# Differential attention and retention with paired score tiles: two products in one two-bank PSUM tile, one VectorE operation for both

## The chip, the core and the metric

The kernel runs on one core of a Trainium2 chip as one program. The metric is the device time of one execution in microseconds (us). The core has five engines with queues of their own: TensorE (matmuls, PE in the profile, its weight loads PEld), VectorE (DVE), ScalarE (ACT), GpSimd (POOL) and SyncE (SP, which issues most of the transfers). Matmuls write to PSUM, eight banks of 128 partitions by 512 float32 elements; VectorE and ScalarE read them from there. A wait between engines goes by semaphore.

## The reference

Two transformer blocks over 512 tokens of width 1024. The first has stick-breaking attention, a gated linear scan and a mixture of 16 experts; the second has retention and differential attention side by side, cross attention and a feed-forward layer. The change touches the second block's mixer alone. Cut to that:

```python
def retention_chunkwise(q, k, v):            # 8 heads, 64 wide, chunks of 128
    scores = einsum('bhncd,bhnjd->bhncj', qc, kc) * dmask      # gamma^(row-column), 0 above the diagonal
    o_intra = einsum('bhncj,bhnjv->bhncv', scores, vc)
    ...                                       # states of earlier chunks, with the same decay
def diff_attention_causal(q, k, v, lam):     # 4 heads, two maps m of 64 each, values 128 wide
    def block(args):                          # a block of 128 queries
        s = einsum('bhmqd,bhmkd->bhmqk', q_blk, k) * scale
        s = where(kpos[None, :] <= qpos[:, None], s, -inf)
        p = softmax(s, axis=-1)
        a = p[:, :, 0] - lam * p[:, :, 1]
        return einsum('bhqk,bhkd->bhqd', a, v)
```

Both results are normalized by head, scaled and multiplied by w_out_2.

## The kernel before

The body is written as one straight program; a scheduler then sets the order of the instructions on each engine, by its own estimate of when operands and buffers are ready, and puts in the semaphores. So projections written behind a head in the program stand between that head's operations on TensorE's queue.

A projection (ws or ts, L192 to L250) takes 512 KB of weights. SP loads them into one of three wraw buffers, ScalarE rounds them to whi (L169), VectorE forms the remainder wlo (L170), and TensorE multiplies three times for each 128 rows of the contraction (L187, L188, L189), into one of two PSUM banks with the tag mm. Sums over squares for the norms are matmuls with ones (L306).

PSUM is split for the whole program: two banks mm, two banks tp, four banks at (L109 and L110). The mixer of the second block runs in two parts.

- diff_head(h), L1175 to L1209, four times. For each of four blocks i of 128 queries, with n = 128(i+1) keys: for each of the two maps m, a score product of 64 partitions into its own bank (L1182), where map 0 has partitions 0 to 63 of query and key and map 1 has 64 to 127; a matmul of the identity with the mask, both bfloat16, which adds -1e30 above the diagonal in the same bank (L1184); the maximum (L1186), its negation (L1187), the exponential with its sum on ScalarE (L1189), the reciprocal (L1190). Then the two maps are weighted and subtracted (L1193, L1194), transposed into another bank (L1197), copied to SBUF (L1199) and multiplied with the values (L1201).
- ret_pair(t), L1256 to L1279, four times, two heads each. For each of four chunks of keys j: two score products, one head in partitions 0 to 63 and one in 64 to 127 (L1266), each multiplied by its decay on VectorE (L1269), and two products with the values (L1271), which write output partitions 0 to 63 and 64 to 127.

float32 matmuls such as these show as two records each in the profile. Queries, keys and values sit in slot2 tiles, 16 buffers with one tag. The rotary step of retention (L1232 to L1240) swaps halves by transfer (sw) and multiplies on VectorE.

Of the kernel before, what the change touches and what calls it, by code (L numbers as in the profile page):

```python
# [8 lines left out]
F32 = mybir.dt.float32  # L9
F32R = mybir.dt.float32r  # L10
BF = mybir.dt.bfloat16
U8 = mybir.dt.uint8
I32 = mybir.dt.int32
AF = mybir.ActivationFunctionType
OP = mybir.AluOpType
AX = mybir.AxisListType.X
PSUM = bass.MemoryType.PSUM
# [3 lines left out]
S = 512  # L21
# [62 lines left out]
def body(tc, a, out):  # L84
# [21 lines left out]
    ps = pool("ps", 1, space=PSUM)  # L106
    dp = pool("dp", 1, space=DRAM)

    def psum(tag, name="ps"):  # L109
        return ps.tile([128, 512], F32, name=name, tag=tag, bufs={"mm": 2, "at": 4, "tp": 2}[tag])  # L110

# [190 lines left out]
    def sums(tag, ones, *sq):  # L302
        w = sq[0].shape[1]
        m = psum(tag)[:, :w]
        for i, q in enumerate(sq):
            T.matmul(m, ones, q, start=(i == 0), stop=(i == len(sq) - 1))  # L306
        return m
# [41 lines left out]
    order(V.tensor_copy(negsb, cs("neg_sb")), last_lo[0])  # L349
    negdf = cp.tile([128, 128], BF, name="negdf")  # L350
    order(V.tensor_copy(negdf, cs("neg_df")), last_lo[0])
# [781 lines left out]
    def slot2(name, dt=F32):  # L1133
        return mp.tile([128, S], dt, name=name, tag="s2", bufs=16)

# [3 lines left out]
    def tmp_(name, bufs):  # L1139
        return tb.tile([128, S], F32, name=name, tag=name, bufs=bufs)  # L1140

    w2 = a["w_in_2"][0]
# [32 lines left out]
    def diff_head(h):  # L1175
        oT = psum("tp")
        for i in range(4):
            n = 128 * (i + 1)
            pp, st = [], []
            for m in range(2):  # L1180
                o = psum("at")[:, :n]
                T.matmul(o, dqn[h][64 * m:64 * m + 64, i * 128:(i + 1) * 128], dkn[h][64 * m:64 * m + 64, :n],  # L1182
                         start=True, stop=False)
                T.matmul(o[:, n - 128:], identb, negdf, start=False, stop=True)  # L1184
                mx_ = sp.tile([128, 3], F32, name="dmx", bufs=6)
                V.reduce_max(mx_[:, 0:1], o, axis=AX)  # L1186
                V.tensor_scalar(mx_[:, 0:1], mx_[:, 0:1], -1.0, None, op0=OP.mult)  # L1187
                p = tmp_("pp", 4)[:, :n]
                A.activation(p, o, AF.Exp, bias=mx_[:, 0:1], accum_out=mx_[:, 1:2])  # L1189
                V.reciprocal(mx_[:, 2:3], mx_[:, 1:2])  # L1190
                pp.append(p)
                st.append(mx_)
            V.tensor_scalar(pp[1], pp[1], st[1][:, 2:3], lam, op0=OP.mult, op1=OP.mult)  # L1193
            V.scalar_tensor_tensor(pp[0], pp[0], st[0][:, 2:3], pp[1], op0=OP.mult, op1=OP.subtract)  # L1194
            pt = psum("at")[:, :n]
            for j in range(i + 1):
                T.transpose(pt[:, j * 128:(j + 1) * 128], pp[0][:, j * 128:(j + 1) * 128], ident)  # L1197
            aT = tmp_("aT", 2)[:, :n]
            A.copy(aT, pt)  # L1199
            for j in range(i + 1):  # L1200
                T.matmul(oT[:, i * 128:(i + 1) * 128], dvn[j][:, h * 128:(h + 1) * 128], aT[:, j * 128:(j + 1) * 128],  # L1201
                         start=(j == 0), stop=(j == i))
        rb = rms_bcast(sq_sums("at", onesr, oT, "hsq"), 128, tb, rbufs=1, name="hrb")
        y = tmp_("hsq", 1)
        V.scalar_tensor_tensor(y, oT, gdf[:, h:h + 1], rb, op0=OP.mult, op1=OP.mult)
        for i in range(2):
            mx[i][4 + h] = mp.tile([128, S], F32R, name="mxd", tag="mxd", bufs=8)
        hilo(mx[0][4 + h], mx[1][4 + h], y)
# [47 lines left out]
    def ret_pair(t):  # L1256
        o = psum("tp")
        hs = [slice(64 * h, 64 * h + 64) for h in range(2)]
        dec = [tmp_("dec", 2) for _ in range(2)]
        for h in range(2):  # L1260
            A.activation(dec[h], rel, AF.Exp, scale=float(np.float32(math.log1p(-2.0 ** (-5.0 - 2 * t - h)))))
        for j in range(4):
            n = S - 128 * j
            p = [psum("at")[:, :n] for _ in range(2)]
            for h in range(2):
                T.matmul(p[h], rk_[t][hs[h], j * 128:(j + 1) * 128], rq[t][hs[h], j * 128:], start=True, stop=True)  # L1266
            w = [tmp_("pp", 4)[:, :n] for _ in range(2)]
            for h in range(2):
                V.tensor_mul(w[h], p[h], dec[h][:, :n])  # L1269
            for h in range(2):  # L1270
                T.matmul(o[hs[h], 128 * j:], rv[j][:, (2 * t + h) * 64:(2 * t + h + 1) * 64], w[h],  # L1271
                         start=(j == 0), stop=(j == 3))
        rb = rms_bcast(sq_sums("at", ones64r, o, "hsq"), 64, tb, rbufs=1, name="hrb")
        y = tmp_("hsq", 1)
# [7 lines left out]
    for c in (0, 2):  # L1282
# [7 lines left out]
        for t in (c, c + 1):  # L1290
            ret_pair(t)
    tst.close()

    xp2 = ExitStack()
# [120 lines left out]
    ts(a["w_down_2"][0], NH, 512, 4, aT, ev_out(512), by_token=False, tag=["mm", "mm", "tp", "tp"])  # L1415
    fst.close()
    xp2.close()
    kvst.close()
# [26 lines left out]
```

## Time and profile before

| | us |
|---|---|
| runs | 1643.37, 1640.85, 1863.65 |
| median of the three | 1643.37 |
| profiled execution | 1641.05 |
| its span, first to last instruction | 1639.3 |
| TensorE busy | 1602.2 |
| VectorE busy | 960.2 |
| ScalarE busy | 833.1 |

The table is read so: the span is one core's; a busy time is the sum of an engine's instructions in it, where overlapping matmuls count once. TensorE is busy for nearly the whole span, the others for about half of it. The rows on which the prediction rests stand in a section of their own below.

### The profile page before, as it was taken

The page shows a single profiled execution, that of the slowest core. Times are in us where ns is not written, and L with a number is a line of the kernel's source. Part 1 is how long each engine was busy: PE and PEld are TensorE (multiplying, and loading weights), DVE is VectorE, ACT ScalarE, POOL GpSimd, SP SyncE. Part 2 cuts the span into 40 slices and gives each one's busy share as a digit, 9 for nine tenths or more (in the row PEclk, how much of TensorE's full clock was granted, in tenths as well). Part 3 has the DMA queues.
Part 4 walks back from the last instruction along what each step waited for, and adds up shares of the span by engine and source line. Part 5 has one row for each costly group of instructions (what it writes and reads, how often), then busy time and mean ns, then how long its engine had stood idle before and what let it go on. Part 6 is the DMA issues. An engine that isn't in the chain of part 4 may idle for free. (4 is left out here: it accounts for less than half of the span.)

```text
span 1639.3 us, 20501 instructions
## 1 busy us (share of the span) xinstructions
PE 1602.2 (98%) x7663; PEld 1234.2 (75%) x7663; DVE 960.2 (59%) x1533; ACT 833.1 (51%) x1331; POOL 74.6 (5%) x92
## 2 busy tenths in 40 slices
PE   7999999999999999999999999999999999999999
PEld 6887776678878777777677667558778888888887
DVE  6459945543647999999865656456654433333221
ACT  5445557565335888888765545425444423222120
POOL 3000000000001211110010000000000000000000
PEclk9999999999999999999999999999999999999999
DMA  7230121123479999999954213124311433333241
GB/s 230 66 103 27 57 82 30 52 93 101 141 244 328 342 370 362 368 361 364 371 192 136 64 52 91 45 71 128 91 52 52 116 103 91 103 91 103 91 128 39
DMA packets 203071, 242.89 MB, mean 148 GB/s; under 512 B 10400, under 2 KB 133560, under 8 KB 202968
## 3 DMA queue, kind: packets, MB, share of 16 engines
q1 hardware_dynamic: 188800, 205.43, 37.7%
q0 software_dynamic: 7056, 24.27, 5.3%
q10 hardware_dynamic: 7112, 11.85, 2.4%
q8 instruction: 61, 1.00, 0.2%
q14 instruction: 42, 0.34, 0.1%
HBM read 223.69 MB, written 15.73 MB: 146 GB/s over the span
## 5 line engine op out<-in xcount | busy, mean ns | idle before, releaser
L170 DVE TENSOR_TENSOR wlo<-wraw,whi 128x1024 fp32r<-128x1024 f32 x210 | 256.1, 1223 | 287.2 <-ACT whi L169 277.3
L169 ACT CAST whi<-wraw 128x1024 fp32r<-128x1024 f32 x210 | 220.5, 1051 | 387.6 <-PE ps L188 263.5
L187 PE MATMUL ps<-hTh,whi 128*128 128x512 f32 (+1 forms) x912 | 349.6, 384 | 1.3 <-DVE fsg L1396 0.8
L188 PE MATMUL ps<-hTl,whi 128*128 128x512 f32 (+1 forms) x912 | 348.2, 382 | 0.9 <-DVE hTl L254 0.9
L189 PE MATMUL ps<-hTh,wlo 128*128 128x512 f32 (+1 forms) x912 | 347.5, 381 | 0.0
L170 DVE TENSOR_TENSOR wlo<-rx,whi 128x1024 fp32r<-128x1024 f32 x176 | 210.8, 1221 | 33.9 <-ACT whi L169 32.6
L169 ACT CAST whi<-rx 128x1024 fp32r<-128x1024 f32 x176 | 183.2, 1049 | 51.6 <-PE ps L189 39.1
L187 PEld LDWEIGHTS ps<-hTh,whi 128*128 128x128 f32 x912 | 172.2, 189 | 34.1 <-issue 1.5
L188 PEld LDWEIGHTS ps<-hTl,whi 128*128 128x128 f32 x912 | 172.1, 189 | 33.3 <-issue 1.6
L189 PEld LDWEIGHTS ps<-hTh,wlo 128*128 128x128 f32 x912 | 172.1, 189 | 31.8 <-issue 0.9
L187 PE MATMUL ps<-whi,XT 128*96 128x512 f32 x256 | 102.0, 398 | 1.8 <-ACTq L1032 1.8
L189 PE MATMUL ps<-whi,XT 128*96 128x512 f32 x256 | 102.5, 400 | 0.0
L188 PE MATMUL ps<-wlo,XT 128*96 128x512 f32 x256 | 101.4, 396 | 0.0
L189 PE MATMUL ps<-whi,hTl 128*128 128x512 f32 x192 | 77.2, 402 | 0.0
L187 PE MATMUL ps<-whi,hTh 128*128 128x512 f32 x192 | 76.5, 398 | 0.3 <-ACT hTh L253 0.2
L188 PE MATMUL ps<-wlo,hTh 128*128 128x512 f32 x192 | 76.6, 399 | 0.0
L187 PE MATMUL ps<-whi,aTh 128*128 128x512 f32 x176 | 68.5, 389 | 0.0
L188 PE MATMUL ps<-wlo,aTh 128*128 128x512 f32 x176 | 68.5, 389 | 0.0
L189 PE MATMUL ps<-whi,aTl 128*128 128x512 f32 x176 | 68.5, 389 | 0.0
L1396 DVE TENSOR_TENSOR fsg<-fsg,ps 128x512 f32<-128x512 f32 x22 | 15.1, 688 | 76.0 <-PE ps L189 76.0
L187 PEld LDWEIGHTS ps<-whi,XT 128*96 128x96 f32 x256 | 41.7, 163 | 18.7 <-ACTq L1032 2.2
L188 PEld LDWEIGHTS ps<-wlo,XT 128*96 128x96 f32 x256 | 41.7, 163 | 17.4
(450 smaller groups left out, 2630.9 us busy)
## 6 DMA issues: line engine op xcount, KB each, us to landing
wraw<-in_w_in_dram SPq DMA_DIRECT2D x72, 512.0 KB
rx<-in_w_exp_gate_dram SPq DMA_DIRECT2D x58, 512.0 KB
rx<-in_w_exp_down_dram SPq DMA_DIRECT2D x58, 512.0 KB
rx<-in_w_exp_up_dram SPq DMA_DIRECT2D x52, 512.0 KB
wraw<-in_w_gate_dram SPq DMA_DIRECT2D x22, 512.0 KB
wraw<-in_w_up_dram SPq DMA_DIRECT2D x22, 512.0 KB
wraw<-in_w_down_dram SPq DMA_DIRECT2D x22, 512.0 KB
wraw<-in_w_out_dram SPq DMA_DIRECT2D x16, 512.0 KB
```

The lines of the kernel that those rows point to most:

```text
L169: i1 = A.copy(hi, w)
L170: i2 = V.tensor_sub(lo, w, hi.bitcast(F32))
L187: T.matmul(o, lh, rh, start=first, stop=False)
L188: T.matmul(o, lh, rl, start=False, stop=False)
L189: T.matmul(o, ll, rh, start=False, stop=last)
L1396: V.tensor_mul(sg[t], sg[t], o)
```

## The change

The four at banks are given out anew for each part of the program: as four single banks before the mixer of the second block and after it, and as two tiles of two banks each (tag at2) during it. A score pair goes into one such tile, one half in each bank.

In the differential heads the mask matmul is gone. The mask is now a float32 tile, and VectorE adds it to the last 128 columns of both halves at once, in place in PSUM. Maximum, negation and reciprocal each run once for both halves; the two exponentials stay two. The transposes go back into the first bank of the same pair. In retention one VectorE product covers both heads, and the two decay tables lie in one tile. The sums of squares of both parts take a pair tile too. The slot2 buffers go from 16 to 15; the probabilities have three pair buffers in place of four single ones.

The scheduler sets the order anew in these two parts. At three places it stands so.

TensorE in the first differential head, at its third block, before (ps<-dk,dq is a score product, negdf the mask, ident,pp a transpose, aT,dv the product with the values, hTh and hTl the activations of a projection):

```order
L1197 MATMUL ps<-ident,pp 128x128 x2
L1182 MATMUL ps<-dk,dq 128x384
L1184 LDWEIGHTS identb
L1184 MATMUL ps<-negdf,identb 128x128
L1182 MATMUL ps<-dk,dq 128x384
L1201 MATMUL ps<-aT,dv 128x128 x2
L1184 LDWEIGHTS identb
L1184 MATMUL ps<-negdf,identb 128x128
L187 MATMUL ps<-hTh,whi 128x512
```

and now:

```order
L1213 MATMUL ps_8516<-ident,pp 128x128 x2
L1200 MATMUL ps_8535<-dk,dq 128x384 x2
L1217 MATMUL ps<-aT,dv 128x128 x2
L1200 MATMUL ps_8556<-dk,dq 128x512 x2
L200 MATMUL ps<-hTh,whi 128x512
```

The two score products of a block stand next to each other, and those of the fourth block follow two output products later. Fourteen projection matmuls come behind them, and then the transposes of the third block.

VectorE at the same place, before (dmx holds maximum, negated maximum, sum and reciprocal; raw, sql and wlo belong to projections):

```order
L170 TENSOR_TENSOR wlo<-wraw,whi 128x1024
L254 TENSOR_TENSOR sql<-sq,sqh 128x512
L1186 TENSOR_REDUCE dmx<-ps 128x1
L1187 TENSOR_SCALAR dmx<-dmx 128x1
L1186 TENSOR_REDUCE dmx<-ps 128x1
L1187 TENSOR_SCALAR dmx<-dmx 128x1
L1190 RECIPROCAL dmx<-dmx 128x1 x2
L1193 TENSOR_SCALAR pp<-pp,dmx,lam 128x384
L1194 SCALAR_TENSOR_TENSOR pp<-pp,dmx 128x384
```

and now:

```order
L1172 COPY raw<-ps 128x512
L183 TENSOR_TENSOR wlo<-wraw,whi 128x1024
L1201 TENSOR_TENSOR ps_8535<-ps_8535,negdf 128x2x128
L267 TENSOR_TENSOR sql<-sq,sqh 128x512
L1203 TENSOR_REDUCE dmx<-ps_8535 128x2
L1201 TENSOR_TENSOR ps_8556<-ps_8556,negdf 128x2x128
L1204 TENSOR_SCALAR dmx<-dmx 128x2
L1203 TENSOR_REDUCE dmx<-ps_8556 128x2
L1208 RECIPROCAL dmx<-dmx 128x2
L1204 TENSOR_SCALAR dmx<-dmx 128x2
L1209 TENSOR_SCALAR pp<-pp,dmx,lam 128x384
L1210 SCALAR_TENSOR_TENSOR pp<-pp,dmx 128x384
```

Two reductions with a negation each have become an addition in PSUM and one reduction, and the addition and the reduction of the fourth block now stand among the steps of the third.

TensorE in retention, third pair (t = 2), before (rq,rk is a score product, pp,rv the product with the values, mxd the projection by w_out_2):

```order
L1266 MATMUL ps<-rq,rk 128x512 x2
L1271 MATMUL ps<-pp,rv 64x512 x2
L1266 MATMUL ps<-rq,rk 128x384 x2
L1266 MATMUL ps<-rq,rk 128x256
L1271 MATMUL ps<-pp,rv 64x384
L1266 MATMUL ps<-rq,rk 128x256
L1271 MATMUL ps<-pp,rv 64x384
L1266 MATMUL ps<-rq,rk 128x128 x2
L1271 MATMUL ps<-pp,rv 64x256 x2
L187 MATMUL ps<-whi,mxd 128x512
L1271 MATMUL ps<-pp,rv 64x128 x2
```

and now:

```order
L1282 MATMUL ps_9795<-rq,rk 128x512 x2
L1282 MATMUL ps_9802<-rq,rk 128x384 x2
L200 MATMUL ps<-whi,mxd 128x512
L1286 MATMUL ps<-pp,rv 64x512 x2
L1282 MATMUL ps_9809<-rq,rk 128x256 x2
L201 MATMUL ps<-wlo,mxd 128x512
L1286 MATMUL ps<-pp,rv 64x384 x2
L1282 MATMUL ps_9816<-rq,rk 128x128 x2
L202 MATMUL ps<-whi,mxd 128x512
L1286 MATMUL ps<-pp,rv 64x256 x2
L1286 MATMUL ps<-pp,rv 64x128 x2
```

Each score pair and each output pair now stands together, and three projection matmuls stand between them where one stood.

The diff, cut to its core:

```diff
@@ -105,9 +105,22 @@
     hp = pool("hp", 1)
     ps = pool("ps", 1, space=PSUM)
     dp = pool("dp", 1, space=DRAM)
+    banks = [ExitStack(), None]
+
+    def four_banks(name, pairs=0):
+
+        banks[0].close()
+        banks[1] = (pool(name, 1, space=PSUM, stack=banks[0]), 4 - 2 * pairs, pairs)
+
+    four_banks("at0")
 
     def psum(tag, name="ps"):
-        return ps.tile([128, 512], F32, name=name, tag=tag, bufs={"mm": 2, "at": 4, "tp": 2}[tag])
+        if tag == "at":
+            return banks[1][0].tile([128, 512], F32, name=name, tag="at", bufs=banks[1][1])
+        return ps.tile([128, 512], F32, name=name, tag=tag, bufs=2)
+
+    def psum2():
+        return banks[1][0].tile([128, 2, 512], F32, name="ps2", tag="at2", bufs=banks[1][2])
 
     def new_hT():
         return (hp.tile([128, 8, S], F32R, name="hTh"), hp.tile([128, 8, S], F32R, name="hTl"))
@@ -301,7 +314,7 @@
 
     def sums(tag, ones, *sq):
         w = sq[0].shape[1]
-        m = psum(tag)[:, :w]
+        m = psum2()[:, 0, :w] if tag == "at2" else psum(tag)[:, :w]
         for i, q in enumerate(sq):
             T.matmul(m, ones, q, start=(i == 0), stop=(i == len(sq) - 1))
         return m
@@ -347,7 +360,7 @@
     order(V.tensor_copy(identb, ident), last_lo[0])
     negsb = cp.tile([128, 128], BF, name="negsb")
     order(V.tensor_copy(negsb, cs("neg_sb")), last_lo[0])
-    negdf = cp.tile([128, 128], BF, name="negdf")
+    negdf = cp.tile([128, 128], F32, name="negdf")
     order(V.tensor_copy(negdf, cs("neg_df")), last_lo[0])
     strictb = cp.tile([128, 128], BF, name="strictb")
     order(V.tensor_copy(strictb, cs("strict")), last_lo[0])
@@ -1131,13 +1144,18 @@
     mx = ([None] * 8, [None] * 8)
 
     def slot2(name, dt=F32):
-        return mp.tile([128, S], dt, name=name, tag="s2", bufs=16)
+        return mp.tile([128, S], dt, name=name, tag="s2", bufs=15)
 
     tst = ExitStack()
     tb = pool("tb", 1, side="right", stack=tst)
 
     def tmp_(name, bufs):
         return tb.tile([128, S], F32, name=name, tag=name, bufs=bufs)
+
+    four_banks("at1", 2)
+
+    def pair_(name, bufs):
+        return tb.tile([128, 2, S], F32, name=name, tag=name, bufs=bufs)
 
     w2 = a["w_in_2"][0]
     dqn, dkn, dvn = {}, {}, {}
@@ -1176,31 +1194,29 @@
         oT = psum("tp")
         for i in range(4):
             n = 128 * (i + 1)
-            pp, st = [], []
+            o = psum2()
             for m in range(2):
-                o = psum("at")[:, :n]
-                T.matmul(o, dqn[h][64 * m:64 * m + 64, i * 128:(i + 1) * 128], dkn[h][64 * m:64 * m + 64, :n],
-                         start=True, stop=False)
-                T.matmul(o[:, n - 128:], identb, negdf, start=False, stop=True)
-                mx_ = sp.tile([128, 3], F32, name="dmx", bufs=6)
-                V.reduce_max(mx_[:, 0:1], o, axis=AX)
-                V.tensor_scalar(mx_[:, 0:1], mx_[:, 0:1], -1.0, None, op0=OP.mult)
-                p = tmp_("pp", 4)[:, :n]
-                A.activation(p, o, AF.Exp, bias=mx_[:, 0:1], accum_out=mx_[:, 1:2])
-                V.reciprocal(mx_[:, 2:3], mx_[:, 1:2])
-                pp.append(p)
-                st.append(mx_)
-            V.tensor_scalar(pp[1], pp[1], st[1][:, 2:3], lam, op0=OP.mult, op1=OP.mult)
-            V.scalar_tensor_tensor(pp[0], pp[0], st[0][:, 2:3], pp[1], op0=OP.mult, op1=OP.subtract)
-            pt = psum("at")[:, :n]
+                ms = slice(64 * m, 64 * m + 64)
+                T.matmul(o[:, m, :n], dqn[h][ms, i * 128:(i + 1) * 128], dkn[h][ms, :n], start=True, stop=True)
+            V.tensor_add(o[:, :, n - 128:n], o[:, :, n - 128:n], negdf[:, None, :].to_broadcast([128, 2, 128]))
+            st = sp.tile([128, 2, 3], F32, name="dmx", bufs=4)
+            V.reduce_max(st[:, :, 0], o[:, :, :n], axis=AX)
+            V.tensor_scalar(st[:, :, 0], st[:, :, 0], -1.0, None, op0=OP.mult)
+            pp = pair_("pp", 3)[:, :, :n]
+            for m in range(2):
+                A.activation(pp[:, m], o[:, m, :n], AF.Exp, bias=st[:, m, 0:1], accum_out=st[:, m, 1:2])
+            V.reciprocal(st[:, :, 2], st[:, :, 1])
+            V.tensor_scalar(pp[:, 1], pp[:, 1], st[:, 1, 2:3], lam, op0=OP.mult, op1=OP.mult)
+            V.scalar_tensor_tensor(pp[:, 0], pp[:, 0], st[:, 0, 2:3], pp[:, 1], op0=OP.mult, op1=OP.subtract)
+            pt = o[:, 0, :n]
             for j in range(i + 1):
-                T.transpose(pt[:, j * 128:(j + 1) * 128], pp[0][:, j * 128:(j + 1) * 128], ident)
+                T.transpose(pt[:, j * 128:(j + 1) * 128], pp[:, 0, j * 128:(j + 1) * 128], ident)
             aT = tmp_("aT", 2)[:, :n]
             A.copy(aT, pt)
             for j in range(i + 1):
                 T.matmul(oT[:, i * 128:(i + 1) * 128], dvn[j][:, h * 128:(h + 1) * 128], aT[:, j * 128:(j + 1) * 128],
                          start=(j == 0), stop=(j == i))
-        rb = rms_bcast(sq_sums("at", onesr, oT, "hsq"), 128, tb, rbufs=1, name="hrb")
+        rb = rms_bcast(sq_sums("at2", onesr, oT, "hsq"), 128, tb, rbufs=1, name="hrb")
         y = tmp_("hsq", 1)
         V.scalar_tensor_tensor(y, oT, gdf[:, h:h + 1], rb, op0=OP.mult, op1=OP.mult)
         for i in range(2):
@@ -1256,21 +1272,20 @@
     def ret_pair(t):
         o = psum("tp")
         hs = [slice(64 * h, 64 * h + 64) for h in range(2)]
-        dec = [tmp_("dec", 2) for _ in range(2)]
+        dec = pair_("dec", 1)
         for h in range(2):
-            A.activation(dec[h], rel, AF.Exp, scale=float(np.float32(math.log1p(-2.0 ** (-5.0 - 2 * t - h)))))
+            A.activation(dec[:, h], rel, AF.Exp, scale=float(np.float32(math.log1p(-2.0 ** (-5.0 - 2 * t - h)))))
         for j in range(4):
             n = S - 128 * j
-            p = [psum("at")[:, :n] for _ in range(2)]
+            p = psum2()[:, :, :n]
             for h in range(2):
-                T.matmul(p[h], rk_[t][hs[h], j * 128:(j + 1) * 128], rq[t][hs[h], j * 128:], start=True, stop=True)
-            w = [tmp_("pp", 4)[:, :n] for _ in range(2)]
+                T.matmul(p[:, h], rk_[t][hs[h], j * 128:(j + 1) * 128], rq[t][hs[h], j * 128:], start=True, stop=True)
+            w = pair_("pp", 3)[:, :, :n]
+            V.tensor_mul(w, p, dec[:, :, :n])
             for h in range(2):
-                V.tensor_mul(w[h], p[h], dec[h][:, :n])
-            for h in range(2):
-                T.matmul(o[hs[h], 128 * j:], rv[j][:, (2 * t + h) * 64:(2 * t + h + 1) * 64], w[h],
+                T.matmul(o[hs[h], 128 * j:], rv[j][:, (2 * t + h) * 64:(2 * t + h + 1) * 64], w[:, h],
                          start=(j == 0), stop=(j == 3))
-        rb = rms_bcast(sq_sums("at", ones64r, o, "hsq"), 64, tb, rbufs=1, name="hrb")
+        rb = rms_bcast(sq_sums("at2", ones64r, o, "hsq"), 64, tb, rbufs=1, name="hrb")
         y = tmp_("hsq", 1)
         V.scalar_tensor_tensor(y, o, col("group_scale_2", t), rb, op0=OP.mult, op1=OP.mult)
         V.tensor_mul(y, y, rg[t])
@@ -1290,6 +1305,7 @@
         for t in (c, c + 1):
             ret_pair(t)
     tst.close()
+    four_banks("at2")
 
     xp2 = ExitStack()
     xp = pool("xp2", 1, side="right", stack=xp2)
@@ -1414,6 +1430,7 @@
     ts(a["w_down_2"][0], NH, 0, 4, aT, ev_out(0), by_token=False, tag="at")
     ts(a["w_down_2"][0], NH, 512, 4, aT, ev_out(512), by_token=False, tag=["mm", "mm", "tp", "tp"])
     fst.close()
+    banks[0].close()
     xp2.close()
     kvst.close()
     es.close()
```

## Rows read from the trace of the kernel before

**Rows 1.** The page: TensorE's busy time, and its granted clock in 40 slices

```profile
PE 1602.2 (98%) x7663; PEld 1234.2 (75%) x7663; DVE 960.2 (59%) x1533; ACT 833.1 (51%) x1331; POOL 74.6 (5%) x92
...
PEclk9999999999999999999999999999999999999999
```

**Rows 2.** Busy time by stretch (the heads): us, engines, clock, DMA

```profile
895.00:1016.00 121.00, 120.81 (x539) 84.41 (x538) 75.44 (x175) 62.78 (x137) 0.00 (x0) 1.00 0.23 64
```

**Rows 3.** The chain of waits by line, 895 to 1016 us

```profile
by line: PE ps L188 20.3%; PE ps L187 20.3%; PE ps L189 20.2%; PE ps L1182 19.4%; PE ps L1201 8.7%; PE ps L1197 4.2%; PE ps L306 3.9%; PE ps L1184 3.1%; issue 0.2%
```

**Rows 4.** Pieces of that chain: start us, us, engine, tile, line, records

```profile
914.59 1.05 PE ps L1182 x2
...
918.53 0.23 PE ps L188
...
924.74 0.91 PE ps L1201 x8
...
928.29 0.41 PE ps L1182 x2
928.71 0.16 PE ps L1184
...
933.86 0.63 PE ps L1182 x2
...
941.54 0.84 PE ps L1182 x2
```

**Rows 5.** Pieces of the chain in retention, pairs 2 and 3

```profile
1082.33 1.18 PE ps L1266 x4
...
1084.24 1.67 PE ps L1271 x4
1085.91 0.90 PE ps L1266 x4
...
1088.88 0.79 PE ps L1271 x2
1089.67 0.42 PE ps L1266 x4
1090.09 0.58 PE ps L1271 x4
...
1091.11 0.37 PE ps L1271 x4
...
1093.75 1.05 PE ps L1266 x2
...
1102.80 0.37 PE ps L1271 x4
```

**Rows 6.** Waits of TensorE, 890 to 1135: us, times, longest

```profile
PE ps L1271 <- DVE pp L1269: 2.5, 5, 1.1
```

**Rows 7.** Groups by shape, 890 to 1135: busy us, mean ns, idle before

```profile
L170 DVE TENSOR_TENSOR wlo<-wraw,whi 128x1024 fp32r<-128x1024 f32 x26 | 31.6, 1222 | 20.5 <-ACT whi L169 20.4
...
L1189 ACT ACTIVATION_READ_ACCUMULATOR pp<-ps,dmx 128x1 f32 x32 | 6.3, 197 | 0.0
...
L1186 DVE TENSOR_REDUCE dmx<-ps 128x1 f32<-128x512 f32 x8 | 5.5, 688 | 9.9 <-PE ps L1184 9.9
...
L1269 DVE TENSOR_TENSOR pp<-ps,dec 128x512 f32<-128x512 f32 x8 | 5.3, 687 | 5.1 <-PE ps L1266 5.1
...
L1190 DVE RECIPROCAL dmx<-dmx 128x1 f32<-128x1 f32 x32 | 5.0, 158 | 9.3 <-ACT pp L1189 9.3
...
L1189 ACT ACTIVATE pp<-ps,dmx 128x384 f32<-128x384 f32 x8 | 4.6, 580 | 9.2 <-DVE dmx L1187 8.4 <-DVE dmx L1190 0.7
...
L1269 DVE TENSOR_TENSOR pp<-ps,dec 128x256 f32<-128x256 f32 x8 | 3.2, 418 | 2.0 <-PE ps L1266 2.0
...
L1194 DVE SCALAR_TENSOR_TENSOR pp<-pp,dmx 128x384 f32<-128x384 f32 x4 | 2.5, 616 | 0.1
...
L1193 DVE TENSOR_SCALAR pp<-pp,dmx,lam 128x384 f32<-128x384 f32 x4 | 1.9, 479 | 0.1
```

## The prediction, made before the changed kernel ran

> **What bounds the kernel now.** I read the page first, then the stretches by engine, then the chain of waits piece by piece, then the groups by shape. The page shows TensorE busy for 98% of the span at a granted clock of nine tenths or more in every slice [rows 1], that is its higher level, 2.4 GHz, from beginning to end. What the change touches lies between 895 and 1016 us (the four differential heads, L1176 to L1209) and from 1035.8 to 1060 and 1082.3 to 1106 us (the four pairs of retention). In the first stretch TensorE is busy for 120.81 of 121 us, VectorE for 75.44 and ScalarE for 62.78, at clock 1.00 [rows 2]. Projections of w_in_2 (L187 to L189) are interleaved with the heads and hide their latency; each of these 512-column matmuls takes 0.23 us of the chain [rows 4]. So time is won only by taking work off TensorE's queue, and lost by anything that opens a hole in it. Idle time of VectorE costs nothing unless TensorE is next.
>
> **The change, part by part.**
>
> *Mask off TensorE.* The 32 identity matmuls and their weight loads (L1184) go. They are 3.1% of the chain of 121 us [rows 3]: 3.75 us; one alone takes 0.16 us [rows 4].
>
> *The two score products come together.* Before, a mask stands between the halves of a pair. One half costs 0.41, 0.63, 0.84 and 1.05 us for 128 to 512 columns [rows 4], 2.93 in all, and 8 halves of each make the 19.4% of 121 us that L1182 has [rows 3]: 23.5 us. In the changed order the halves are neighbours. Retention shows what that is worth: its products have the same shapes (64 partitions, one half in each), and two that stand together (four records) take 0.42 for 128 columns, 0.90 for 384, and 1.18 for 512 after a wait, where a 512 alone takes 1.05 [rows 5]. So neighbours run side by side and a pair costs hardly more than one half. With 0.24 us per 128 columns between the 128 and the 384, a set of four pairs costs 0.42 + 0.66 + 0.90 + 1.14 = 3.12 us, four heads 12.5 us. This takes off 23.5 - 12.5 = 11 us, with the masks 14.75 us.
>
> *VectorE in the heads.* Added are 16 adds of 2x128 elements in PSUM. No operation of before writes PSUM from VectorE; the nearest rows are the product out of PSUM with 256 elements, 0.42 us, and that with 512, 0.69 [rows 7]. I take 0.42, the same count of elements, and keep 0.3 and 0.7 as ends (0.3 is the same 0.27 us per 256 elements with hardly any fixed part). Reductions, negations and reciprocals fall from 32 to 16 each: two of 0.69 become one of 1.22 (0.27 us per further 256 elements), and a reciprocal of 0.16 goes per pair, the negation is as small [rows 7]. Sixteen of each save about 2.4 us three times, the adds cost 6.7: VectorE's sum stays where it was. Its sequence is what changes. Before, the first half was reduced and exponentiated while TensorE still worked on the second. Now the add waits for both, the reduction is twice as long, and both exponentials wait for it.
>
> *Holes in TensorE's queue.* I walk the third block of the first head in the changed order, from the start of its score pair (t = 0), with the durations of [rows 7]; there an operation of VectorE over 512 elements takes 0.69. TensorE: pair of 384 columns to 0.90, two output products (eight records, which are four products, take 0.91 [rows 4], so 0.23 each), pair of 512 to 2.5, fourteen projections to 5.7; then the transposes of the third block stand in the queue. VectorE: ahead of the add stand a copy of 512 elements (0.69) and a weight remainder of 1.22, done at 1.6; add to 2.0, a remainder of 512 elements (0.69) to 2.7, maximum over 768 elements (0.96) to 3.65, the add of the fourth block to 4.1, negation to 4.25. ScalarE: two exponentials of 0.58 with their 0.20 reads, to 5.9. VectorE: reciprocal, the fourth block's negation, 0.48 and 0.62 for the weighting, to 7.4. The transposes start at 7.5: a hole of 1.8 us. The fourth block then finds 2.2 us of cover more and comes in time. The first two blocks lose 0.4. The second head, walked in the same way, loses 0.8, 0.35, 1.3 and 0.1. The third and fourth have fewer evacuations on VectorE and hold fewer projections. I take 2.5 us a head, 10 us in all; ends 2 (the projections cover nearly all) and 32 (2 us in each of 16 blocks). The ends of the add, 0.3 and 0.7, move this by -2 to +4 us, since it stands once in each block's sequence.
>
> *Retention.* TensorE waited 2.5 us for the decay products on VectorE (L1269) [rows 6]. Now one product serves both halves, so the two output products become ready together. Before, one 384 alone took 0.79, and four records of 256 and of 128, both halves ready, 0.58 and 0.37; but the 512s, the second half late, 1.67 [rows 5]. At 0.21 us per 128 columns, 512 together is 1.00. Pair 2 took from 1082.33 to 1091.48 us, 9.15 with one projection inside. Changed: scores to 1.18 and 2.08, a projection, one product of 1024 elements (1.22) done at 2.5, outputs 2.6 to 3.6, scores of 256 to 4.3, a projection. VectorE meanwhile does two rotary products of 512 elements (0.69 each) and the 768-element one to 4.8; outputs 4.9 to 5.7, scores of 128, a projection, outputs of 256 and 128 to 7.3. That holds three projections; net of them 6.6 against 8.9: 2.3 us won. Pair 0 is built alike. Pairs 1 and 3 took 9.42 us with two projections from 1093.75 to 1103.17 [rows 5]; the same walk gives 8.7 with four, as the sum of squares still splits their 512 scores: 1.2 won. Together 7 us; ends 3 (only the waits of rows 6 go) and 10.
>
> *Edits at no cost.* One slot2 buffer fewer (15): the fourth rv takes the slot of a query that head 0 has finished with; by then TensorE has the projections, and without that cover it would be one wait of at most a head. Pools of PSUM open and close where the banks have been idle for long. The mask's copy at the start stands beside weight loads. The sum of squares takes a pair slot: the next head's second block waits for its logarithm, under four projections. SP's and GpSimd's queues keep their order.
>
> **Sum.** -14.75 + 10 - 7 = -11.75 us. The profiled execution ran 1641.05 us (span 1639.3, and 1.75 around it), 2.3 below the median of the runs shown, 1643.37. So 1629.3, rounded to 1629. A difference under 2% of about 1640, 33 us, counts as no change here, and this is 0.7%.
>
> **Rivals.**
>
> *Full gain.* The projections cover everything: -21.75, 1619 us. For it: before, the same kind of sequence left only 0.19 us of 121 idle [rows 2]. Against: the walk finds 1.8 us at one place, and TensorE now reaches the transposes earlier.
>
> *VectorE and ScalarE become the bound of the heads* (slower). Only two pairs of banks exist, and a pair is held from its scores until the copy of its transposes. If every block waits for add, maximum, exponentials and weighting in turn, the point from which that decides is 21.75 / 16 = 1.4 us per block; at 2 us it is +10, 1651 us. For it: the holes of 1.8 and 1.3 us in the walk. Against: VectorE's 75 us are well under the some 106 that the heads would take, and the walk finds other blocks with 0.1. The Trainium skill has this as a rule (TensorEngine Tiling (Array Packing), Performance Considerations, PSUM Bottleneck): side-by-side matmuls speed up TensorE but not the evacuation of PSUM, which may become the bottleneck. By that rule alone it would be the 1651 us of this rival; the busy times bear it out only in single blocks so far.
>
> *The pairs do not run side by side.* Then only 3.75 of 14.75 us go, but TensorE also comes later to each transpose and the holes shrink to about 1: -3.75 + 1 - 7 = -9.75, 1631 us. The time could not tell it from the forecast, the pieces of the chain would.
>
> **Chances.** Forecast (1622 to 1638) 0.62; full gain 0.15; VectorE bound 0.15; not side by side 0.05; something unseen 0.03. The range 1616 to 1647 takes in the forecast with the ends of its unknown terms, most of the full gain (0.04 left below) and about half of the slower rival (0.08 above). Over 2% faster would need 33 us where 22 are to be had: 0.02. Over 2% slower needs over 3 us of hole in every block: 0.03. Within: 0.95.
>
> **What would show it.** In the profile after: no L1184; a pair of scores (four records) at 0.4 to 1.2 us of the chain, or at twice that if the third rival is right; the added operation in PSUM near 0.42 us; TensorE's wait for L1210 (transposes for the weighting) near 10 us in the heads, near 0 for the full gain, over 22 for the slower rival; the wait for the decay products gone from 2.5 us to about 1; outputs of 512 at 1.0. The prediction is wrong if TensorE's time in the heads does not fall by some 15 us less the holes, or if the time moves outside these stretches, where the order is the same.

## The result, and where the time went

The changed kernel takes 1623.19 us (median of 4 runs, 1622.06 to 1623.45); the kernel before took 1643.37 beside it (three runs; a fourth of 1863.65 us is a slow one and is left out). The ratio is 0.9879, with a 95% interval from 0.9860 to 0.9899: 1.2% faster, inside the 2% that counts as no change here. A second comparison on another chip gave 0.9878 (0.9856 to 0.9900). The profiled execution took 1623.13 us, its span 1621.3.

The page after, TensorE's line and its granted clock, answers to [rows 1]:

```profile
PE 1579.7 (97%) x7631; PEld 1223.8 (75%) x7631; DVE 955.9 (59%) x1485; ACT 831.6 (51%) x1331; POOL 75.2 (5%) x92
...
PEclk9999999999999999999999999999999999999999
```

32 records (the masks) are gone, and TensorE is busy for 22.5 us less. VectorE and ScalarE are as busy as they were. So the time was won on TensorE's queue, and the next two fences say in which stretch. They give the busy time by stretch, first of before, then of after: from the first score of the heads to the first score of retention, and from there to the end of retention's last output (columns: stretch, us, PE, PEld, DVE, ACT, POOL, clock, DMA share, GB/s; in brackets the number of records).

```profile
897.50:1035.80 138.30, 138.11 (x619) 98.57 (x618) 82.30 (x183) 72.67 (x152) 0.00 (x0) 1.00 0.24 69
1035.80:1103.20 67.40, 64.27 (x261) 35.63 (x260) 35.76 (x61) 22.17 (x33) 0.00 (x0) 1.00 0.19 55
```

```profile
899.70:1024.50 124.80, 123.42 (x589) 91.02 (x588) 80.83 (x151) 71.92 (x152) 0.00 (x0) 1.00 0.27 76
1024.50:1085.30 60.80, 57.88 (x266) 34.03 (x265) 33.72 (x45) 21.97 (x33) 0.00 (x0) 1.00 0.22 61
```

The heads shrink by 13.5 us with the same 384 projections in both, retention by 6.6 with five more matmuls inside (266 records against 261). What comes after retention lasts 536.1 and 536.0 us, no change. The clock is at its higher level in all four stretches (1.00). Elsewhere it falls for a few us in both kernels, which a slice of 40 us on the page does not show: before, the mean is 0.62 from 866.0 to 870.5 us, and in the changed kernel it is 0.52 here, behind a wait of 3.50 us that ended at 845.63:

```profile
847.50:851.00 3.50, 3.50 (x9) 2.63 (x9) 2.97 (x5) 2.39 (x6) 0.00 (x0) 0.52 0.96 272
```

The heads begin 2.2 us later than before. Part of that is scatter, as in another execution of the same changed kernel they begin at 897.9. But the two profiles of this study with the heads of before begin them at 897.5, and the ten with changed heads at 897.9 to 902.5, although TensorE's order up to there is the same. A transfer that the work ahead waits for (xa_d<-XG, issued near 821 us) takes 5.3 and 5.6 us in the two and 6.1 to 8.6 in the ten; whether the change has a part in that is not shown. For this reason the lengths of the two stretches are compared below rather than single end times.

Where a stretch's time goes is best read from starts. For every matmul record I took the time from its start to the next record's start, put the idle time that the row names apart, and added up by kind. In the heads (us):

| | before | after | halves in the same rows |
|---|---|---|---|
| scores | 23.51 | 11.79 | 20.16 |
| masks | 3.04 | 0 | 0 |
| projections | 91.16 | 92.96 | 92.07 |
| transposes | 5.42 | 3.58 | 3.44 |
| products with values | 9.91 | 9.79 | 9.92 |
| sums of squares | 5.26 | 5.45 | 5.32 |
| idle | 0 | 1.23 | 0 |
| stretch | 138.30 | 124.80 | 130.91 |

and in retention, from the first score to the start of the record behind the last output:

| | before | after | decay by halves | scores early |
|---|---|---|---|---|
| scores | 15.12 | 12.92 | 14.65 | 10.84 |
| outputs | 16.55 | 10.57 | 15.30 | 10.58 |
| projections and sums | 32.46 | 34.33 | 35.93 | 33.74 |
| idle | 3.13 | 2.93 | 2.17 | 2.95 |
| stretch | 67.26 | 60.75 | 68.05 | 58.11 |

(The last columns are experiments 3, 4 and 8.) The score pairs gave 11.7 us, the masks 3.0, retention's outputs 6.0 and its scores 2.2. Two shifts in the heads that were not forecast, 1.8 less at the transposes and 1.8 more at the projections, cancel.

The pieces of the chain of waits show the pairs (start us, us, engine, tile, line, records), with four records to a pair, where [rows 4] had two to a half:

```profile
921.70 0.42 PE ps L1200 x4
...
924.18 0.63 PE ps L1200 x4
...
929.17 0.84 PE ps L1200 x4
...
955.36 1.06 PE ps L1200 x4
```

A pair costs what one half cost before (0.41, 0.63, 0.84, 1.05): the second half is free. The added operations of VectorE, by shape, where [rows 7] had single halves (the numbers behind the shape: busy us, mean ns, idle before):

```profile
L1201 DVE TENSOR_TENSOR ps<-ps,negdf 128x256 f32<-128x256 f32 x16 | 6.7, 421 | 0.6 <-PE ps L1200 0.6
...
L1284 DVE TENSOR_TENSOR pp<-ps,dec 128x1024 f32<-128x1024 f32 x4 | 4.9, 1223 | 6.5 <-PE ps L1282 6.5
L1203 DVE TENSOR_REDUCE dmx<-ps 128x2 f32<-128x1024 f32 x4 | 4.9, 1222 | 0.0
```

The add in PSUM takes 0.421 us, where 0.42 was forecast, and the maximum of 1024 elements the 1.22 that the prediction took for two of 0.69. TensorE's waits from 880 to 1125 us (us in all, times, longest), beside the 2.5 us of [rows 6]:

```profile
PE ps L1286 <- DVE pp L1284: 1.7, 4, 0.9
...
PE ps L1213 <- DVE pp L1210: 1.2, 3, 0.6
```

The last row is the term that the forecast put at 10 us.

Retention in the chain, pairs 2 and 3, answers to [rows 5]:

```profile
1067.11 1.14 PE ps L1282 x4
1068.28 1.24 DVE pp L1284
1069.56 1.08 PE ps L1286 x4
1070.63 0.63 PE ps L1282 x4
...
1071.69 0.80 PE ps L1286 x4
...
1076.66 1.05 PE ps L1282 x2
1077.71 0.43 PE ps L319
1078.14 1.07 PE ps L1282 x2
1079.23 1.24 DVE pp L1284
1080.51 1.08 PE ps L1286 x4
```

A pair of 512 outputs takes 1.08 us, where it took 1.67 with the second half late. In the fourth pair the sum of squares (L319) still stands between the two score halves, and each costs its 1.05 again; experiment 8 is about that.

### The profile page after: what moved, and what is told of

It is laid out like the page before. It is cut to its first block, busy times and chain, and to the rows that moved or that the text cites. A ratio compares the mean times of both kernels' runs of the same rounds, so it can differ in the third digit from the quotient of the medians.

```text
span 1621.3 us, 20374 instructions
## 1 busy us (share of the span) xinstructions
PE 1579.7 (97%) x7631; PEld 1223.8 (75%) x7631; DVE 955.9 (59%) x1485; ACT 831.6 (51%) x1331; POOL 75.2 (5%) x92
```

## The experiments

The theory: nearly all of the gain is that two half-height products stand next to each other on TensorE's queue, in different rows (scores) or columns (outputs), and that VectorE's longer sequence is paid in cover (projections that TensorE works on while a block's sequence runs), because the order on the queue puts projections where a block waits. The rivals: that it is the masks and waits that went and not the concurrency, and that VectorE's sequence costs time in every block.

**1 and 2. Each part alone.** The heads changed and retention with single banks and a decay product for each half:

```diff
-            p = psum2()[:, :, :n]
+            p = [psum("at")[:, :n] for _ in range(2)]
...
-            V.tensor_mul(w, p, dec[:, :, :n])
+            for h in range(2):
+                V.tensor_mul(w[:, h], p[h], dec[:, h, :n])
```

> The differential heads as in the change, retention with its four single banks and one product of VectorE per half as before (both halves written into one tile of probabilities). Theory: the two parts add up; from the first score product of the heads to the first of retention TensorE needs 124.8 us in the changed kernel and 138.3 before, so this kernel is some 13.5 us faster than before, near 1629.5, and retention takes again some 67 us. Rival (the gain is one of the scheduler's arrangement or of the start of the stage, not of the parts): no such split, anything between 1621 and 1641.

Measured: 1631.92 us, ratio 0.9932 (0.9916 to 0.9949). Retention changed and the heads as before:

```diff
-            o = psum2()
             for m in range(2):
+                o = psum("at")[:, :n]
...
+                T.matmul(o[:, n - 128:], identb, negdf, start=False, stop=True)
...
-            V.tensor_add(o[:, :, n - 128:n], o[:, :, n - 128:n], negdf[:, None, :].to_broadcast([128, 2, 128]))
```

> Retention as in the change, the differential heads as before (four single banks, mask by matmul, one reduction per half). Theory: only retention's 6 to 8 us are won, near 1636, and the heads take again some 138 us. Rival: as for heads_only. Together the two gains should make the 20 us of the whole within 2 us if the parts are independent.

Measured: 1635.67 us, ratio 0.9957 (0.9943 to 0.9971). Against the 1643.54 us of before on that chip these are -11.6 and -7.9, together -19.5, and the whole change gave -20.2 against its own before: the parts add up within the scatter. The heads alone have the changed kernel's stretch (124.9 us against 124.8), but their retention lasts 69.4 us where before had 67.3, which is most of the 2.4 us by which the kernel came out above what was expected. Of these 2.1 us, 1.5 come from a stretch at the lower clock in the third pair, behind waits of 1.12 and 0.78 us; before has no such stretch in retention:

```profile
1074.50:1078.00 3.50, 3.50 (x8) 1.13 (x7) 1.39 (x3) 0.00 (x0) 0.00 (x0) 0.51 0.03 9
```

The 512 outputs take 2.56 us there where before took 1.67, and the next scores 1.53 where it took 0.90.

**3. Halves in the same rows.** Both halves read partitions 0 to 63, so the second map is not computed and the first one stands in its place; TensorE's order is the changed kernel's, instruction for instruction:

```diff
-                ms = slice(64 * m, 64 * m + 64)
+                ms = slice(0, 64)
```

> The changed kernel, but both score products of a block in the heads take map 0, so both sit in partitions 0 to 63 (map 1 is left out of the computation). Every instruction, its size and its place on every queue stay as in the change. Theory (neighbours in different partitions run side by side): each set of four pairs costs 5.9 us instead of 3.1, 11 us for four heads, less the holes that close (about 1): near 1633. A pair of 512 columns takes about 2 us in the chain. Rival 1 (the gain of the pairs is only that no 128-row matmul stands between the halves): no slower than 2 us, near 1624. Rival 2 (VectorE and ScalarE set the pace of the heads): the time does not change.

Measured: 1629.34 us, ratio 0.9919 (0.9902 to 0.9935), 6.15 above the changed kernel. Pieces of its chain:

```profile
923.10 0.64 PE ps L1200 x4
925.80 1.06 PE ps L1200 x4
931.14 1.48 PE ps L1200 x4
934.80 1.91 PE ps L1200 x4
```

So 5.09 us for the four pairs of a head where the changed kernel takes 2.95. The starts show the concurrency directly: in the first 384 pair of the changed kernel the records of the two halves start 0.007 us apart, two by two, and here all four start 0.32 to 0.43 us apart. The table by starts tells what the time alone would hide. Working in different rows is worth 8.4 us of scores (20.16 against 11.79). The other 3.35 us up to the 23.51 of before go with being neighbours, without concurrency; no run has the halves apart throughout with no mask between them, so the mask's part in it is not shown. And since TensorE now comes later to each transpose, the idle 1.23 us vanish and 0.9 of the projections with them, which is why the time rises by 6 and not by 8.4. The expectation of 1633 had left out the neighbours' part.

**4. Decay by halves.** The pair tile stays, VectorE multiplies each half by its decay on its own:

```diff
-            V.tensor_mul(w, p, dec[:, :, :n])
+            for h in range(2):
+                V.tensor_mul(w[:, h], p[:, h], dec[:, h, :n])
```

> The changed kernel, but retention's decay product is again one operation of VectorE per half, in the same pair tiles. Theory: the second half is ready 0.3 to 0.6 us after the first, so the two output products of 512 and 384 columns no longer start together; they cost 1.7 and 1.3 us instead of 1.07 and 0.80, some 4 us over four pairs, of which the earlier start gives part back: 2 to 4 us slower than the change. Rival (only the number of VectorE operations or the waits count): under 1 us, or faster because the first half is ready earlier.

Measured: 1631.29 us, ratio 0.9928 (0.9911 to 0.9944), 8.1 above the changed kernel and twice the upper end of what was expected. Pieces of its chain, pair 2:

```profile
1071.86 0.70 DVE pp L1285
1072.61 1.07 PE ps L1287 x2
1073.68 0.43 PE ps L200
...
1074.57 1.00 PE ps L1287 x2
1075.57 0.63 PE ps L1282 x4
```

The first half's product is ready 0.5 us earlier, its output starts at once, and projections fill the time until the second half: 1.07 + 1.00 us of outputs in place of 1.08. In the table the outputs go from 10.57 to 15.30, the scores from 12.92 to 14.65 (their order changes too), while TensorE idles less than in the changed kernel (2.17 against 2.93). So one VectorE operation for both halves gains nothing by being shorter on VectorE; it makes the two operands ready at one moment, and with that the two outputs neighbours. This is most of the gain in retention: the stretch takes 68.05 us, with ten more projections inside, where before took 67.26.

**5 and 6. VectorE's sequence shorter and longer.** No mask in the heads at all, and the mask added three times:

```diff
-            V.tensor_add(o[:, :, n - 128:n], o[:, :, n - 128:n], negdf[:, None, :].to_broadcast([128, 2, 128]))
```

> Leaves the mask of the heads out altogether; the rest is the changed kernel. Theory (TensorE's order puts as many projections ahead of each block's transposes as VectorE's sequence needs, so a step there is paid in cover and not in time): the order holds 173 projections ahead of the last score pair where the changed kernel holds 201, the waits of the transposes, 1.2 us in the changed kernel, stay between 0.5 and 2, and the time is 1622 to 1624. Rival (the prediction's walk, by which each block's sequence on VectorE is late by 0.1 to 1.8 us): every block loses 0.34 us or more of its sequence, 16 blocks 5.4 us, 1618.

Measured: 1625.32 us (1621.36 to 1626.61), ratio 0.9872 (0.9856 to 0.9889). The time missed its band by 1.3 us, in the direction away from the rival. The idle time of its heads is 0.3 us, 1 less than in the changed kernel, but in its own order two pairs of scores stand apart (13.09 us of scores in place of 11.79): that costs what the shorter sequence gives.

> Adds the mask of the heads three times; two more adds of 0.34 us from start to start in each of 16 blocks, 11 us of VectorE. Theory: paid in cover, 247 projections ahead of the last score pair in place of 201, none of 384 added; waits of the transposes 1 to 2 us; time 1623 to 1625. Rival (VectorE's sequence decides in each block): 11 us, 1634.

Measured: 1623.73 us, ratio 0.9870 (0.9853 to 0.9886). 32 more adds are 11 us of VectorE and cost nothing that can be measured; the heads last 124.5 us, 0.64 of them idle:

```profile
PE ps L1215 <- DVE pp L1212: 0.6, 2, 0.3
```

**7. Beyond the cover.** The mask added six times.

> Adds the mask of the heads six times; five more adds, 1.7 us a block and 27 us of VectorE, more than the 1.4 us a block from which the prediction's slower rival decides. Theory: still paid in cover, 307 projections ahead of the last score pair of the 384 that there are; waits of the transposes 1 to 3 us; time 1623 to 1627. Rival: 27 us, 1650.

Measured: 1640.17 us (1637.35 to 1642.83), ratio 0.9968 (0.9955 to 0.9981): 17 above the changed kernel. Neither theory had it right. The heads last 141.5 us, and the loss is in one place, the second head (the four begin at 902.5, 935.5, 972.5 and 1006.5 us), as TensorE's rows there show (start us, us, line, shapes, idle before and what ended it):

```profile
939.89 0.40 PE L202 MATMUL ps<-whi,hTl 128*128 128x512 f32 x1
944.04 0.45 PE L1218 MATMUL ps<-ident,pp 128*128 128x128 f32 x1 [3.75 <-DVE dmx L1209]
...
959.75 0.87 PE L1218 MATMUL ps<-ident,pp 128*128 128x128 f32 x3 [3.15 <-DVE pp L1215]
...
963.07 0.63 PE L200 MATMUL ps<-whi,hTh 128*128 128x512 f32 x1
```

Between the projections that start at 939.89 and at 963.07 us there is none. They have not been used up: 120 of the 384 have run by then, and 264 follow. What they lack is a PSUM bank. Each output tile of the projections (24 matmuls) takes one of the two mm banks, and both are held by tiles that ScalarE has still to read. VectorE copied the first of them, a key, at 931.19 us; ScalarE squares it 30 us later, and copies the second, a value of retention, later still (start us, us, shapes, idle before; copies and squares paired by their order):

```profile
961.37 0.60 ACT L1165 ACTIVATE sq<-ps 128x512 f32<-128x512 f32 x1 [0.23 <-DVE sql L267]
...
970.34 0.57 ACT L1246 COPY rv<-ps 128x512 f32<-128x512 f32 x1
```

The next projection starts 1.1 us after the square has ended. In the same stretch of the changed kernel a square starts 0.7 to 1.5 us after VectorE's copy. ScalarE is not short of time, with 6.64 us of work from 940 to 960; the order on its queue sets the square behind other steps, and why it does so is not shown, nor did a run give the projections a third bank. TensorE is idle for 9.5 us there (10.1 in all heads), and its granted clock falls. The same stretch by pieces:

```profile
940.00:945.00 5.00, 0.89 (x4) 0.34 (x2) 3.93 (x14) 1.74 (x8) 0.00 (x0) 0.83 0.00 0
945.00:950.00 5.00, 5.00 (x11) 2.29 (x12) 1.58 (x5) 0.63 (x3) 0.00 (x0) 0.50 0.01 3
```

Behind the wait of 3.75 us it is 0.50, that is 1.2 GHz. From 950 to 960 us its mean lies between the levels (0.65 and 0.69), from 960 to 965 it is 0.50 again, and from 970 it is back at 1.00. Of the 16.7 us that the stretch grew, 8.9 are idle time and 7.8 are records that took longer from start to start, by the clock or because the new order splits pairs (scores 3.2 more, sums 1.3, products with values 1.3, transposes 1.1, projections 0.8). So 0.67 us more per block is free, and 1.7 stalls the covering projections in one head out of four, where the price then comes at once; no run lies between the two.

**8. Scores ahead of the sums.** In the changed kernel the sum of squares of one retention pair stands between the two 512 scores of the next. Here pair 1 and pair 3 issue these scores first:

```diff
+        if t % 2 == 0:
+            first[t + 1] = ret_scores(t + 1, 0)
         rb = rms_bcast(sq_sums("at2", ones64r, o, "hsq"), 64, tb, rbufs=1, name="hrb")
```

> The 512 scores of retention pairs 1 and 3 are issued before the sum of squares of the pair ahead, so that the sums no longer stand between their halves. Theory (halves run side by side only as neighbours): 1.05 + 0.42 + 1.07 us become about 1.15 + 0.25 + 0.2, 0.9 to 1.3 us each, twice: 1620.5 to 1621.5. Rival (VectorE's rotary products and decay products decide there, TensorE then waits): 1623, with 1 to 2 us more of waiting for L1292's operand.

Measured: 1619.88 us, ratio 0.9846 (0.9829 to 0.9862). The medians of the two kernels came from different chips, so both ran again on one, in five rounds.

> The changed kernel once more, for the comparison with the next one on the same chip: 0.986 to 0.990 of the time before.

> The scores of retention pairs 1 and 3 ahead of the sums, against the changed kernel on the same chip. Theory (the sums stood between two halves that now run side by side, with fewer returns to projections): 2.5 to 3.5 us below the changed kernel, as the stretch of retention shortened by 2.6 us in the profile. Rival (the 3.3 us between the medians came from two chips): within 1 us of it.

Measured: 1623.10 us for the changed kernel and 1620.77 with the scores early (0.9878, 0.9856 to 0.9900, and 0.9859, 0.9836 to 0.9881). The 2.3 us lie between the two expectations and the intervals overlap, so the times alone do not decide. The stretch does: retention lasts 58.1 us in both profiles with the scores early, and 60.75 and 60.3 in the two of the changed kernel; 2.1 us of that are scores (10.84 against 12.92). This is the fastest kernel of the study. Its fourth pair:

```profile
1074.90 0.50 PE ps L319
...
1077.05 1.01 PE ps L1292 x4
1078.06 1.28 PE ps L1277 x8
```

The 512 scores are done before the sums, and behind the outputs two more pairs (384 and 256 columns, eight records) run on in 1.28 us.

## Why the prediction held, and where it was off

The forecast was 1629 with a range of 1616 to 1647, and the time is 1623, inside. The gain is 17.9 us between the profiled executions (with the heads beginning 2.2 us late in the second) and 20.2 between the medians, where 11.75 were forecast. Point by point:

- *TensorE bounds these stretches.* Right: VectorE got 11 us of added work in experiment 6, and the time did not move. That the clock is at its higher level from beginning to end was read from slices of 40 us and is not so (0.62 from 866.0 to 870.5 us before); the stretches of the sum are at 1.00.
- *Masks, -3.75.* Measured -3.0 by starts.
- *Score pairs, -11.* Measured -11.7. The reading of retention's neighbours in [rows 5] gave the right price before any head had run so. Experiment 3 shows what it consists of: 8.4 us of concurrency, and 3.35 that go with being neighbours. The third rival (not side by side) is out; the pieces tell it, as the prediction said they would, and not the time.
- *The add, 0.42.* Measured 0.421.
- *Holes in TensorE's queue, +10.* This is the term that was mis-sized: 1.2 us measured, three waits. The walk of the first head's third block can be laid beside the chain through that block, from the start of its score pair at 907.93 us:

```profile
908.25 1.23 DVE wlo L183
909.48 0.34 DVE ps L1201
909.82 0.59 DVE sql L267
910.41 0.87 DVE dmx L1203
911.28 0.34 DVE ps L1201
...
911.78 1.24 ACT pp L1207 x4
...
913.27 0.47 DVE pp L1209
...
913.76 0.63 DVE pp L1210
...
914.53 0.52 PE ps L1213 x3
```

The path is the one of the walk, step for step. But the transposes start at 6.6 us after the pair, not at 7.5, and TensorE is done with the projections ahead of them at 6.0, not at 5.7. The walk added durations (0.42, 0.69, 0.96, and 1.56 for two exponentials with their reads), and in a queue each step costs the distance from start to start (0.34, 0.59, 0.87, 1.24), since an operation starts before the one ahead of it has ended by the profile. Over some ten steps that is 0.9 us, half of the hole of 1.8 that the walk found. The other 0.3 are on TensorE: the first projection behind a score pair takes 0.34 us to the next start in place of 0.23, and the last one counts to its end (0.39). The trace has a hole of 0.58. The rest of the error is that this one place was carried over to four heads. In the changed kernel's trace the transposes of all 16 blocks start 0.05 to 0.25 us after the end of their weighting (L1210), yet TensorE waits in only three places out of 16: the order puts as many projections ahead as each block needs. The numbers of the order agree: 173 projections stand ahead of the last score pair without an add, 201 in the changed kernel, 247 with three adds and 307 with six. (They compare only kernels that differ by adds: the order of before, with four single banks, has 277 there.) The walk's surplus of a microsecond looked like a hole in every block only because that order leaves hardly any slack. With 1.2 in place of 10 the sum would have been -20.6.

The overlap could have been read before the run, from two rows of VectorE in the trace of before:

```profile
1079.24 0.69 DVE L1238 TENSOR_TENSOR raw<-raw,tabs 128x512 f32<-128x512 f32 x1 [3.15 <-DMA sw<-raw]
1079.86 0.69 DVE L1239 TENSOR_TENSOR sw<-sw,tabs 128x512 f32<-128x512 f32 x1
```

The second starts 0.62 us after the first, which lasts 0.69. The Trainium skill (VectorE: DVE Perf Modes, The DRAIN you can't avoid) says that the next operation does not start until the pipe is empty, and also that one that is not held starts earlier; these rows show the second case.

- *Retention, -7.* Measured -6.5, or -7.7 net of the five more matmuls at 0.23. The size was right and so was the main reason (outputs together). The other reason given, that the wait for decay products falls from 2.5 to about 1, was weak: it is 1.7, and TensorE's idle time in retention hardly moved (3.13 to 2.93).
- *Rivals.* The full gain, 1619, was nearer to the mark than it was given credit for: only 1.2 of its 21.75 us are missing by the terms, and the time lies at the lower edge of the forecast's own band, 1622 to 1638. VectorE and ScalarE as the bound, with a decision at 1.4 us a block, is no story about this kernel, but experiment 7 shows that the place exists: with 1.7 us a block the gain falls from 20 us to about 4. The way is not the one of the rival, though: the loss is in one head and not spread over all, and it comes when the covering projections wait for their banks. The Trainium skill (TensorEngine Tiling (Array Packing), Performance Considerations, PSUM Bottleneck) says that the copy out of PSUM may become the bottleneck after a fourfold speed-up of TensorE; the pairs here are twofold. The changed kernel does not show it, with 1.2 us of waiting. With six adds the projections do lack banks, but ScalarE, which has to read them, is busy for only a third of that time.

What stays open: whether the later start of the heads belongs to the change, why the order with six adds reads the banks so late, why the transposes cost 1.8 us less and the projections 1.8 more in the changed order, and what of the 0.9 us of projections in experiment 3 belongs to the waits of weight loads.

## What to carry to other kernels

Two products of half the rows or half the columns cost little more than one only as neighbours on TensorE's queue: look for what stands between them, a mask, a sum of squares, or an operand that comes half a microsecond late, and give both operands by one operation. When a chain of small operations is walked by hand, add the distances from start to start, not the durations, and do not multiply a hole found in one block where a planned order fills the queue up to the moment when each block is ready. Ask what the covering work itself needs, here two PSUM banks that VectorE and ScalarE read from the same queues as the longer sequence: a longer sequence costs nothing while they are freed in time, and once they are not, the price comes at once and with a lower clock.

## What the runs showed of the hardware

- Neighbouring products of 64 partitions in the same rows are cheaper than apart with a mask between: pairs of 0.64, 1.06, 1.48 and 1.91 us, where two halves took 0.82 to 2.10; in different rows, 0.42, 0.63, 0.84 and 1.06, with starts 0.007 us apart.
- VectorE adds in place in PSUM across two banks at the price of retention's product out of PSUM with 256 elements, 0.42 us, and 0.33 to 0.34 from start to start.
- With six adds the granted clock was 0.50 behind a wait of 3.75 us on TensorE, in heads that are at 1.00 in the changed kernel, and back at 1.00 from 970 us. It was also low behind a wait of 3.50 us (0.52, in the changed kernel ahead of the heads) and behind waits of 1.12 and 0.78 us close together (0.51, in experiment 1).
